# Score maxima as 128-row products with both groups first, block-diagonal expert keys, first expert product ordered by term

## The chip, the cores and the metric

The program runs on one core of one Trainium2 chip. The metric is the device time of one execution in microseconds (us). The engines are TensorE (PE, with its weight loads as PEld), VectorE (DVE), ScalarE (ACT), GpSimd (POOL) and SyncE (SP), each with an instruction queue of its own that runs in order, and DMA queues.

## What is computed

A two-layer diffusion backbone over 512 latent tokens and 256 context tokens, model width 1024. Cut to what matters here:

```python
for l in range(2):                      # layer 1 ("last") has latent queries only
    h = rms(x) * (1 + s1) + sh1         # modulated by c (latents) or c_ctx (context)
    q, k, v, u = split(h @ w_in[l])     # 8 query heads, 2 key heads, head width 64
    o_attn = softmax(q k^T / 8) v       # latents see context + latents, context sees context
    o_conv = silu(layer_norm(depthwise_conv31(glu(u))))
    x = x + g1 * concat(rms(o_attn), rms(o_conv)) @ w_o[l]
    h = rms(x) * (1 + s2) + sh2
    qp = (h @ w_pq[l]).reshape(T, 8, 2, 64)
    s = einsum('thcd,hckd->thck', qp, sub_keys)          # 2 halves x 128 keys
    i = top 16 of the 16 x 16 sums of the top 16 of each half   # of 16384 experts
    x = x + g2 * sum_e softmax(s_e) * gelu(h . U[e]) * V[e]     # 16 experts x 8 heads a token
return rms(x) * final_g
```

## The kernel before

Tokens lie on the columns: `xT[:, k, t]` holds 128 of the 1024 features of token t. A value that needs more than one pass of precision is split into a rounded part and a rest (`khh`/`klo`, `hhi`/`hlo`, `hi`/`lo`), and a product is the sum of two or three matmuls of the parts.

**Attention.** `att()` is one stream that a merge interleaves with the convolution's blocks (`convs`), the modulation products (`md`, tiles `mp`, `mps`) and the context's projection (`ctx`). For each group of queries, first the context tiles `CT`, then the latent tiles `LAT`, `largest` computes each query's largest score per head: for each head and span of keys one matmul L545 of `khh` over 128 rows and one L546 of `klo` over the lower 64 rows (`HD`), both into tile `s`, and a DVE reduction L547 into `nm`. `max_rows` turns `nm` into rows of `mT`, by way of `mh` on ACT. Then `attend` computes the probabilities from scores the other way round: `sT` is a matmul L435 of `khh` and a matmul L436 of `klo` with `qm`, both over 128 rows. The upper 64 rows of `klo` hold ones (L296), which in L436 subtract the maximum held in `mT`. The exponential is on ACT, the product with the values is `po` (L450). Of the convolution's 31 taps, DVE does some blocks (`L396`) and the pair ACT (`tp`, L399) and POOL (`yT`, L400) the others. `project_ctx` waits until the context's attention is done (`"att"`), and the output projection is `wo` (L676).

**Expert layer.** The 16384 experts are gone through densely for the larger part of the tokens, in 128 chunks a layer. `u_stream` loads a chunk (`raw`, SP's queue), rounds it on ACT (`hi`), takes the rest on POOL (`lo`), and runs 24 matmuls (`ups`, L963): 8 feature blocks times the three terms hi·hhi, hi·hlo, lo·hhi. GELU follows on ACT (`ge`), and the result is written out (`gd`). `v_stream` (`vps`, L1004) does the second product later. Beside `u_stream` run `queries` and `best16`: a projected query (`pq`, ring of tag `t2`) is multiplied with the `keys` (tile `sc`), whose two halves of 64 rows are two matmuls into two PSUM tiles, and DVE takes the 16 largest. `fg_stream` gathers single experts (`uv`) for the other tokens (L878 and L867 on DVE); `w_stream` builds the dense weights (`o`, `wps`).

**Order.** Streams are merged by clocks that add each step's estimated cost; a scheduler then places each engine's instructions in a fixed order in its queue.

Of the kernel before, what the change touches and what calls it, by code (L numbers as in the profile page):

```python
# [9 lines left out]
F32 = mybir.dt.float32  # L10
# [3 lines left out]
AF = mybir.ActivationFunctionType  # L14
# [3 lines left out]
P = 128  # L18
D = 1024
KD = D // P  # L20
SEQ = 512
CTX = 256
T = SEQ + CTX
NL = SEQ // P
NT = T // P
HD = 64
NQ = 8
NKV = 2
# [5 lines left out]
PH = 8  # L34
PK = 128
# [5 lines left out]
NEG = -3.0e38  # L41
# [19 lines left out]
def body(ctx: ExitStack, tc: tile.TileContext, io):  # L61
    nc = tc.nc
# [22 lines left out]
    V.memset(ones, 1.0)  # L85
    cT = per.tile([P, KD, 2], F32, name="cT")
    nc.sync.dma_start(cT, io["cT"])
    xT = per.tile([P, KD, T], F32, name="xT")
    x_src = io["xT"].rearrange("(k p) t -> p k t", p=P)
    for i in list(range(NL, NT)) + list(range(NL)):  # L90
# [9 lines left out]
    iota = per.tile([P, PK], F32, name="iota")  # L100
    V.tensor_copy(iota, iota_i)

    scT = per.tile([P, KD, 32], F32, name="scT")
    V.memset(scT, 0.0)
    A.activation(scT[:, :, 0:2], cT, AF.Silu)
    sel = per.tile([P, 2], F32, name="sel")
    V.tensor_tensor(out=sel, in0=ident[:, 0:2], in1=ident[:, 32:34], op=ALU.add)
    for g in (2, 3):
# [94 lines left out]
    def norm(tiles, hT, bc):  # L203

        t0, n = tiles[0] * P, len(tiles) * P
        for k in range(KD):
            V.tensor_tensor(out=hT[k], in0=xT[:, k, t0:t0 + n], in1=bc, op=ALU.mult)
# [22 lines left out]
    def attention_layer(l, st, fgs, fp, mark):  # L230
# [4 lines left out]
        last = l == 1  # L235
# [57 lines left out]
        klo = kp.tile([P, NKV, T], F32R, tag="klo", name="klo")  # L293
        vv = kp.tile([P, NT, NKV, HD + 1], F32, tag="vv", name="vv")
        V.memset(vv[:, :, :, HD:], 1.0)
        A.copy(klo[HD:], ones[HD:, 0:1].unsqueeze(2).to_broadcast([P - HD, NKV, T]))  # L296
        mT = kp.tile([P, nq * P], F32, tag="mT", name="mT")
        segs = [(0, SEQ, PAD)] if last else [(SEQ, CTX, LSEG + PAD), (0, SEQ, PAD)]
        gw = LSEG if last else GW
# [231 lines left out]
        def largest(g, kts, complete=True):  # L531

            k0, nk = kts[0] * P, len(kts) * P
            nh = max(1024 // nk, 1)
            for i in g:
                ts = slice(i * P, (i + 1) * P)
                nm = sm.tile([P, NQ], F32, tag="nm", name="nm", bufs=6)
                for h in range(0, NQ, nh):
                    ps = pbig.tile([P, 1024], F32, tag="big", name="s")
                    for j in range(nh):  # L540
                        for c in range(0, nk, 512):
                            n = min(512, nk - c)
                            ks = slice(k0 + c, k0 + c + n)
                            o = ps[:, j * nk + c:j * nk + c + n]
                            PE.matmul(o, qs[:, h + j, ts], khh[:, (h + j) % NKV, ks], start=True, stop=False)  # L545
                            PE.matmul(o, qs[0:HD, h + j, ts], klo[0:HD, (h + j) % NKV, ks], start=False, stop=True)  # L546
                    V.tensor_reduce(out=nm[:, h:h + nh], in_=ps[:, 0:nh * nk].rearrange("p (h k) -> p h k", k=nk), axis=AX.X, op=ALU.max, negate=True)  # L547
                    yield 0.9 * nh * nk / 768
                if i in part:
                    V.tensor_tensor(out=nm, in0=nm, in1=part[i], op=ALU.min)  # L550
                part[i] = nm
                if complete:
                    max_rows(i, nm)
# [82 lines left out]
        def att():  # L636
            if not last:
                yield from largest(CT, CT)
                yield from attend(CT, sp)
                done.append("att")  # L640
            yield from largest(LAT, CT[1:] if last else list(range(NT)))
            done.append("max")
            yield from attend(LAT, sp)

        def after_conv():
# [37 lines left out]
    def peer_layer(l, fp):  # L683
# [6 lines left out]
        with ExitStack() as outer:  # L690
# [19 lines left out]
            def best16(tiles, h, qT, keys, tmp):  # L710

                n = len(tiles)
                s = tmp.tile([P, 2, 2, PK], F32, tag="sc", name="sc", bufs=2)
                ps = [prt.tile([P, 2, PK], F32, tag="small", name="sc") for _ in range(2)]
                for c in range(2):
                    cs = slice(c * HD, (c + 1) * HD)
                    for j in range(n):
                        PE.matmul(ps[c][:, j, :], qT[cs, j * P:(j + 1) * P], keys[cs, h, :], start=True, stop=True)
                    A.copy(s[:, c, 0:n], ps[c][:, 0:n])
                for j, i in enumerate(tiles):  # L720
                    top, tix = tops[i]
                    for c in range(2):
                        V.max(out=top[:, h, c, 0:8], in_=s[:, c, j, :])
                        V.max_index(out=tix[:, h, c, 0:8], in_max=top[:, h, c, 0:8], in_values=s[:, c, j, :])
                        V.match_replace(out=s[:, c, j, :], in_to_replace=top[:, h, c, 0:8], in_values=s[:, c, j, :], imm_value=NEG)
                        V.max(out=top[:, h, c, 8:16], in_=s[:, c, j, :])
                        V.max_index(out=tix[:, h, c, 8:16], in_max=top[:, h, c, 8:16], in_values=s[:, c, j, :])

            def queries(g, hT, keys, tmp, first=False):

                n = len(g) * P
                todo = []
                for h in range(PH):
                    w = tmp.tile([P, KD, P], F32, tag="wq", name="wq", bufs=2)
                    nc.gpsimd.dma_start(w, io["peer_wq"][l][:, h * P:h * P + P].rearrange("(k p) n -> p k n", p=P))
                    ps = prt.tile([P, 512], F32, tag="small", name="pqp")
                    if len(hT) == 1:
                        terms = [(w, hT[0])]
                    else:
                        hi = tmp.tile([P, KD, P], F32R, tag="wqh", name="wqh", bufs=2)  # L740
                        lo = tmp.tile([P, KD, P], F32R, tag="wql", name="wql", bufs=2)
                        A.copy(hi, w)
                        G.tensor_tensor(out=lo, in0=w, in1=hi.bitcast(F32), op=ALU.subtract)
                        terms = [(hi, hT[0]), (hi, hT[1]), (lo, hT[0])]
                    for k in range(KD):
                        for m, (a, b) in enumerate(terms):
                            PE.matmul(ps[:, 0:n], a[:, k, :], b[k], start=k == 0 and m == 0, stop=k == KD - 1 and m == len(terms) - 1)
                    q = tmp.tile([P, 512], F32, tag="t2", name="pq", bufs=4)
                    A.copy(q[:, 0:n], ps[:, 0:n])
                    yield 1.0  # L750
                    todo.append((h, q))

                    while len(todo) > (1 if h < PH - 1 else 0):
                        done, q = todo.pop(0)
                        for j in range(0, len(g), 2):
                            best16(g[j:j + 2], done, q[:, j * P:], keys, tmp)
                            yield 2.0 * len(g[j:j + 2])
                        if first and (done + 1) % RH == 0:
                            yield from route(g[0], r2, done + 1 - RH, done + 1)
# [71 lines left out]
            def norm_fg(tmp):  # L831

                n = len(fgt) * P
                v = 0 if fgt[0] < NL else 1
                hT = []
                for _ in range((n + P) // (2 * P)):
                    t = fp.tile([P, 2 * D], F32, tag="g", name="hTf", bufs=4)
                    hT += [t[:, k * n:(k + 1) * n] for k in range(2 * D // n)]
                norm(fgt, hT, rms_rows(fgt, tmp, tag="t2", bufs=4) if l == 0 else rbc[:, td:])
                modulate(l, 1, v, hT)  # L840
                return hT

# [108 lines left out]
            def u_stream():  # L951

                for c in range(PK):
# [4 lines left out]
                    A.copy(hi, raw)  # L958
                    mark.append(G.tensor_tensor(out=lo, in0=raw, in1=hi.bitcast(F32), op=ALU.subtract))  # L959
                    ps = pdd[0].tile([P, 512], F32, tag="dd", name="ups")  # L960
                    for k in range(KD):
                        for n, (a, b) in enumerate(((hi, hhi), (hi, hlo), (lo, hhi))):
                            PE.matmul(ps[:, 0:td], a[:, k, :], b[:, k, :], start=k == 0 and n == 0, stop=k == KD - 1 and n == 2)  # L963
                    ge = up.tile([P, 512], F32, tag="ge", name="ge")
                    A.activation(ge[:, 0:td], ps[:, 0:td], AF.Gelu)  # L965
# [51 lines left out]
            us = u_stream()  # L1017
            fgs = fg_stream()
            with tc.tile_pool(name=f"tmp{l}", bufs=1, reuse_waits="tile") as tmp:
                keys = tmp.tile([P, PH, PK], F32, name="keys")  # L1020
                nc.sync.dma_start(keys, io["keys"][l])
                for i in fgt:
                    tops[i] = (tmp.tile([P, PH, 2, TOPK], F32, name=f"top{i}"), tmp.tile([P, PH, 2, TOPK], U32, name=f"tix{i}"))
                if l == 0:
                    hfg = norm_fg(tmp)
                for k in range(KD):
                    h = tmp.tile([P, 512], F32, tag="t2", name="xn", bufs=4)[:, 0:td]
                    V.tensor_tensor(out=h, in0=xT[:, k, 0:td], in1=rbc[:, 0:td], op=ALU.mult)
                    A.activation(h, h, AF.Identity, bias=mods[l, 3][:, k, 0:1], scale=mods[l, 4][:, k, 0:1])
                    A.copy(hhi[:, k, :], h)  # L1030
                    (G if k % 2 else V).tensor_tensor(out=hlo[:, k, :], in0=h, in1=hhi[:, k, :].bitcast(F32), op=ALU.subtract)  # L1031
# [124 lines left out]
```

## Time and profile before

| what | value |
|---|---|
| time, median of 3 runs | 4389.49 us (4384.52 to 4396.72) |
| the profiled execution: time, span | 4393.92 us, 4391.8 us |
| mean granted TensorE clock | 0.923 of full speed |
| busy: PE, PEld | 3982.1 us (91%), 3276.5 us (75%) |
| busy: DVE, POOL, ACT | 3110.9 us (71%), 2226.0 us (51%), 1901.0 us (43%) |

The span runs from the first to the last instruction of the profiled execution, 2.1 us less than its time, and that execution lies 4.4 us above the median. A busy share is a mean over stages that have different limits, and ends of pipelined matmuls are modelled, so that starts of successive matmuls tell their cost better than their durations.

### The profile page before, as it was taken

To read this page: it belongs to the slowest core of one execution; us is meant where nothing else is said; L and a number is where in the kernel's file an instruction comes from. 1 tells how busy PE (TensorE), PEld (TensorE's weight loads), DVE (VectorE), ACT (ScalarE), POOL (GpSimd) and SP (SyncE) were. 2 spreads that over 40 slices of the span, in tenths; PEclk is the share of its full clock that TensorE was granted. 3 is DMA by queue.
4 is the path that set the end of the run, shared out by engine and by line. 5 is a ranking of instruction groups with operands and counts; after the bars stand their busy time and mean duration, and the time that the engine had idled before them with its cause. 6 is when DMAs were issued, how large, how long until landed. Compare 5 with 4: busy or idle time off the path is not lost.

```text
span 4391.8 us, 54819 instructions
## 1 busy us (share of the span) xinstructions
PE 3982.1 (91%) x19512; PEld 3276.5 (75%) x19512; DVE 3110.9 (71%) x5700; ACT 1901.0 (43%) x3752; POOL 2226.0 (51%) x1231
## 2 busy tenths in 40 slices
PE   8879989999898998999999779889989889899998
PEld 5545857777787776888777535768878888889997
DVE  4683338999888657887877773349898553788886
ACT  3331432334777743333333243434367663333332
POOL 0551033657566455556555264136566455666664
PEclk9955989999999999999999875989999999999998
DMA  5132114797888898989887513226667778778885
GB/s 158 58 125 96 49 51 128 280 336 283 266 285 270 291 330 311 344 327 341 323 336 283 214 44 100 68 80 231 208 211 238 250 250 278 288 291 307 319 317 179
DMA packets 397921, 1003.75 MB, mean 229 GB/s; under 512 B 24400, under 2 KB 239696, under 8 KB 344400
## 3 DMA queue, kind: packets, MB, share of 16 engines
q1 hardware_dynamic: 330176, 577.10, 38.6%
q0 software_dynamic: 59904, 419.46, 25.9%
q10 hardware_dynamic: 7568, 3.70, 0.3%
q8 instruction: 154, 2.52, 0.2%
q14 instruction: 119, 0.97, 0.1%
HBM read 884.29 MB, written 115.87 MB: 228 GB/s over the span
## 4 chain that ended last, share of the span: by engine, by line
PE 37%; DVE 15%; DMA 11%; issue 5%; POOL 3%; ACT 2%; SPq 1%; POOLq 0%; ACTq 0%; DVEq 0%
PE vps L1004 19%; PE ups L963 8%; DMA raw<-in_uT 5%; DMA uv<-in_uv,uix 4%; DVE ge L939 2%; DVE alo L943 2%; PE wps L931 2%; DVE o L925 2%; POOL lo L959 2%; DMA vr<-in_vq 2%; DVE uv L878 1%; DVE yp L867 1%; PE wo L676 1%; PE s L546 1%; PE s L545 1%
## 5 line engine op out<-in xcount | busy, mean ns | idle before, releaser
L959 POOL TENSOR_TENSOR lo<-raw,hi 128x1024 fp32r<-128x1024 f32 x256 | 656.0, 2563 | 551.9 <-ACT hi L958 541.7
L997 POOL TENSOR_TENSOR vlo<-vr,vhi 128x1024 fp32r<-128x1024 f32 x256 | 632.4, 2478 | 476.6 <-ACT vhi L996 455.5
L963 PE MATMUL ups<-hhi,hi 128*128 128x512 f32 (+1 forms) x2048 | 773.8, 379 | 50.5 <-ACT ge L965 24.9
L963 PE MATMUL ups<-hhi,lo 128*128 128x512 f32 (+1 forms) x2048 | 775.7, 379 | 43.7 <-POOL lo L959 43.4
L1004 PE MATMUL vps<-ahi,vhi 128*128 128x512 f32 (+1 forms) x2048 | 756.7, 371 | 32.8 <-ACT vhi L996 19.3
L1004 PE MATMUL vps<-alo,vhi 128*128 128x512 f32 (+1 forms) x2048 | 759.2, 371 | 28.5 <-DVE alo L943 28.5
L963 PE MATMUL ups<-hlo,hi 128*128 128x512 f32 (+1 forms) x2048 | 767.4, 375 | 0.7 <-DVE hlo L1031 0.7
L1004 PE MATMUL vps<-ahi,vlo 128*128 128x512 f32 (+1 forms) x2048 | 750.0, 371 | 3.2 <-POOL vlo L997 3.2
L878 DVE SCALAR_TENSOR_TENSOR uv<-uv,hp 128x1024 f32<-128x1024 f32 x363 | 439.7, 1211 | 240.7 <-DMA uv<-in_uv,uix 240.3
L867 DVE SCALAR_TENSOR_TENSOR yp<-uv,act,yp 128x1024 f32<-128x1024 f32 x359 | 460.3, 1282 | 156.6 <-ACT act L880 151.9
L874 POOL DMA_INDIRECT uv<-in_uv,uix x384 | 434.2, 1131 | 211.7 <-DVE y L867 40.0
L963 PEld LDWEIGHTS ups<-hhi,lo 128*128 128x128 f32 x2048 | 397.4, 194 | 102.3 <-POOL lo L959 60.7
L963 PEld LDWEIGHTS ups<-hhi,hi 128*128 128x128 f32 x2048 | 398.6, 195 | 98.7 <-ACT ge L965 29.3
L1004 PEld LDWEIGHTS vps<-ahi,vhi 128*128 128x128 f32 x2048 | 390.2, 191 | 86.6 <-ACT vhi L996 19.9
L1004 PEld LDWEIGHTS vps<-alo,vhi 128*128 128x128 f32 x2048 | 390.9, 191 | 83.3 <-DVE alo L943 34.9
L1004 PEld LDWEIGHTS vps<-ahi,vlo 128*128 128x128 f32 x2048 | 390.2, 191 | 58.0 <-POOL vlo L997 6.8
L963 PEld LDWEIGHTS ups<-hlo,hi 128*128 128x128 f32 x2048 | 398.5, 195 | 42.7 <-DVE hlo L1031 1.5
L879 ACT ACTIVATE act<-dots 128x1 f32<-128x1 f32 x384 | 77.7, 202 | 790.0 <-DVE uv L878 783.0
L925 DVE TENSOR_TENSOR o<-iota,xf 128x1024 f32<-128x1024 f32 x224 | 375.5, 1698 | 29.7 <-PE wps L931 15.2
L400 POOL TENSOR_TENSOR yT<-yT,tp 128x512 f32<-128x512 f32 (+1 forms) x150 | 252.1, 1681 | 232.0 <-ACT tp L399 215.5
L996 ACT CAST vhi<-vr 128x1024 fp32r<-128x1024 f32 x256 | 266.1, 1045 | 218.6 <-PE vps L1004 103.0
L958 ACT CAST hi<-raw 128x1024 fp32r<-128x1024 f32 x256 | 267.3, 1045 | 186.5 <-DMA raw<-in_uT 97.9
(271 smaller groups left out, 6470.1 us busy)
## 6 DMA issues: line engine op xcount, KB each, us to landing
raw<-in_uT SPq DMA_DIRECT2D x256, 512.0 KB
vr<-in_vq SPq DMA_DIRECT2D x256, 512.0 KB
wd<-sg SPq DMA_DIRECT2D x28, 2048.0 KB
wm<-in_w_mod SPq DMA_DIRECT2D x48, 1024.0 KB
w<-wd SPq DMA_DIRECT2D x32, 1024.0 KB
gd<-ge SPq DMA_DIRECT2D x120, 256.0 KB
ge<-gd SPq DMA_DIRECT2D x60, 512.0 KB
w<-wd SPq DMA_DIRECT2D x32, 768.0 KB
```

The costliest lines, as they stand in the source:

```text
L400: G.tensor_tensor(out=y, in0=y, in1=tp, op=ALU.add)
L867: V.scalar_tensor_tensor(y, t[:, 1, :], act[:, e:e + 1], y, op0=ALU.mult, op1=ALU.add)
L874: got = G.indirect_dma_start(out=t.rearrange("p c d -> p (c d)"), out_offset=None, in_=io["uv"], in_offset=bass.IndirectOffsetOnAxis(ap=ui ...
L878: V.scalar_tensor_tensor(t[:, 0, :], t[:, 0, :], 1.0, at["h"], op0=ALU.mult, op1=ALU.mult, accum_out=dots[:, ec])
L925: V.tensor_tensor(out=oh, in0=iota.unsqueeze(1).unsqueeze(1).to_broadcast([P, 2, 4, PK]), in1=c2[:, :, tt].to_broadcast([P, 2, 4, PK]), op ...
L931: PE.matmul(ps[:, j, :], o1[:, j, :], o2[:, j, :], start=True, stop=True)
L958: A.copy(hi, raw)
L959: mark.append(G.tensor_tensor(out=lo, in0=raw, in1=hi.bitcast(F32), op=ALU.subtract))
L963: PE.matmul(ps[:, 0:td], a[:, k, :], b[:, k, :], start=k == 0 and n == 0, stop=k == KD - 1 and n == 2)
L996: A.copy(vhi, raw)
L997: mark.append(G.tensor_tensor(out=vlo, in0=raw, in1=vhi.bitcast(F32), op=ALU.subtract))
L1004: PE.matmul(ps[:, 0:td], a[:, c % 4, d * P:(d + 1) * P], b, start=c == 0 and n == 0, stop=c == 7 and n == 2)
```

## The change

1. The tile `scT` (SiLU of the two conditioning vectors) is filled before the input loads are issued from ACT's queue, and not after them.
2. `klo`'s upper 64 rows are first written as zeros; `largest` multiplies over all 128 rows in its second matmul too. In layer 0 both groups' maxima come first, then the upper rows are set to ones, then context and latents attend. In layer 1 the order of maxima and attention stays.
3. `keys` becomes block-diagonal: 128 rows, and for each head 256 columns, of which each half of the rows fills 128 and the others are zero. A tile of tokens then takes one matmul in place of two, with one PSUM tile and one copy for both halves. The ring `t2` has three buffers in place of four.
4. `u_stream` runs its 24 matmuls term by term, not feature block by feature block.

```diff
+    scT = per.tile([P, KD, 32], F32, name="scT")
+    V.memset(scT, 0.0)
+    A.activation(scT[:, :, 0:2], cT, AF.Silu)
     xT = per.tile([P, KD, T], F32, name="xT")
...
-    scT = per.tile([P, KD, 32], F32, name="scT")
-    V.memset(scT, 0.0)
-    A.activation(scT[:, :, 0:2], cT, AF.Silu)
...
-        A.copy(klo[HD:], ones[HD:, 0:1].unsqueeze(2).to_broadcast([P - HD, NKV, T]))
+        A.activation(klo[HD:], ones[HD:, 0:1].unsqueeze(2).to_broadcast([P - HD, NKV, T]), AF.Copy, scale=0.0)
...
-                            PE.matmul(o, qs[0:HD, h + j, ts], klo[0:HD, (h + j) % NKV, ks], start=False, stop=True)
+                            PE.matmul(o, qs[:, h + j, ts], klo[:, (h + j) % NKV, ks], start=False, stop=True)
...
             if not last:
                 yield from largest(CT, CT)
+            yield from largest(LAT, CT[1:] if last else list(range(NT)))
+            done.append("max")
+            A.copy(klo[HD:], ones[HD:, 0:1].unsqueeze(2).to_broadcast([P - HD, NKV, T]))
+            if not last:
                 yield from attend(CT, sp)
                 done.append("att")
-            yield from largest(LAT, CT[1:] if last else list(range(NT)))
-            done.append("max")
             yield from attend(LAT, sp)
...
-                ps = [prt.tile([P, 2, PK], F32, tag="small", name="sc") for _ in range(2)]
-                for c in range(2):
-                    cs = slice(c * HD, (c + 1) * HD)
-                    for j in range(n):
-                        PE.matmul(ps[c][:, j, :], qT[cs, j * P:(j + 1) * P], keys[cs, h, :], start=True, stop=True)
-                    A.copy(s[:, c, 0:n], ps[c][:, 0:n])
+                ps = prt.tile([P, 2, 2, PK], F32, tag="small", name="sc")
+                for j in range(n):
+                    PE.matmul(ps[:, j], qT[:, j * P:(j + 1) * P], keys[:, h], start=True, stop=True)
+                A.copy(s[:, 0:n], ps[:, 0:n])
...
-                    q = tmp.tile([P, 512], F32, tag="t2", name="pq", bufs=4)
+                    q = tmp.tile([P, 512], F32, tag="t2", name="pq", bufs=3)
...
-                    for k in range(KD):
-                        for n, (a, b) in enumerate(((hi, hhi), (hi, hlo), (lo, hhi))):
+                    for n, (a, b) in enumerate(((hi, hhi), (hi, hlo), (lo, hhi))):
+                        for k in range(KD):
                             PE.matmul(ps[:, 0:td], a[:, k, :], b[:, k, :], start=k == 0 and n == 0, stop=k == KD - 1 and n == 2)
...
-                keys = tmp.tile([P, PH, PK], F32, name="keys")
-                nc.sync.dma_start(keys, io["keys"][l])
+                keys = tmp.tile([P, PH, 2, PK], F32, name="keys")
+                for c in range(2):
+                    cs = slice(c * HD, (c + 1) * HD)
+                    V.memset(keys[cs, :, 1 - c], 0.0)
+                    nc.sync.dma_start(keys[cs, :, c], io["keys"][l][cs])
```

How the instructions move is shown at three places. A row is line, operation, output<-inputs and the output's shape; line numbers of the changed kernel are one higher at these places.

PE in layer 0, at the end of the context's maxima, before:

```order
L545 MATMUL s<-khh,qs 128x256
L546 MATMUL s<-klo,qs 128x256
L127 MATMUL mp_1283<-wm,scT 32x256 x8
L435 MATMUL sT<-qs,khh 128x256
L139 MATMUL mps<-sel,m_1292 128x2 x2
L127 MATMUL mp_1300<-wm,scT 32x256 x8
```

PE at the same place, in the changed kernel:

```order
L546 MATMUL s<-khh,qs 128x256
L547 MATMUL s<-klo,qs 128x256
L128 MATMUL mp_1283<-wm,scT 32x256 x8
L546 MATMUL s<-khh,qs 128x512
L547 MATMUL s<-klo,qs 128x512
L546 MATMUL s<-khh,qs 128x256
L547 MATMUL s<-klo,qs 128x256
L140 MATMUL mps<-sel,m_1292 128x2 x2
```

The context's attention (`sT` of 256 columns) no longer stands here: the latents' maxima follow at once, and the context's `sT` stand behind the last of them.

DVE in layer 0, from the last of the context's maxima on, before (`nm<-s 128x4` is a maximum of context queries, `128x1` of latent queries, `yT` a tap of the convolution):

```order
L547 TENSOR_REDUCE nm<-s 128x4
L396 SCALAR_TENSOR_TENSOR yT<-gp,convw,yT 128x798
L140 TENSOR_TENSOR mod_2_1246<-mps,bmod 128x4
L561 COPY ng<-mh 128x8
L562 TENSOR_TENSOR ng<-nm,mh 128x8
L396 SCALAR_TENSOR_TENSOR yT<-gp,convw,yT 128x798
L140 TENSOR_TENSOR mod_2_1246<-mps,bmod 128x4
L396 SCALAR_TENSOR_TENSOR yT<-gp,convw,yT 128x798 x2
```

DVE at the same place, in the changed kernel:

```order
L548 TENSOR_REDUCE nm<-s 128x4
L548 TENSOR_REDUCE nm<-s 128x1
L397 SCALAR_TENSOR_TENSOR yT<-gp,convw,yT 128x798
L141 TENSOR_TENSOR mod_2_1246<-mps,bmod 128x4
L562 COPY ng<-mh 128x8
L563 TENSOR_TENSOR ng<-nm,mh 128x8
L548 TENSOR_REDUCE nm<-s 128x1
L397 SCALAR_TENSOR_TENSOR yT<-gp,convw,yT 128x798
L548 TENSOR_REDUCE nm<-s 128x1
```

The taps, which stood in one run with no latent maximum between them, now alternate with the 32 latent maxima, and the last taps stand behind the last maximum.

PE in the expert layer's first product, layer 0, before (`htp` is another stream's transposition):

```order
L1041 MATMUL htp<-ident,hTf 128x128 x8
L963 MATMUL ups<-hhi,hi 128x512
L963 MATMUL ups<-hlo,hi 128x512
L963 MATMUL ups<-hhi,lo 128x512
L963 MATMUL ups<-hhi,hi 128x512
```

PE there in the changed kernel:

```order
L1046 MATMUL htp<-ident,hTf 128x128 x4
L964 MATMUL ups<-hhi,hi 128x512 x8
L964 MATMUL ups<-hlo,hi 128x512 x6
L1046 MATMUL htp<-ident,hTf 128x128 x4
L964 MATMUL ups<-hlo,hi 128x512 x2
L964 MATMUL ups<-hhi,lo 128x512 x6
```

The first matmul that reads `lo` was the third of a chunk's 24 and is now the seventeenth; the last that reads `hi` was the twenty-third and is now the sixteenth.

## Rows read from the trace of the kernel before

**Rows 1.** The page: share of the chain that ended last, by line.

```profile
PE vps L1004 19%; PE ups L963 8%; DMA raw<-in_uT 5%; DMA uv<-in_uv,uix 4%; DVE ge L939 2%; DVE alo L943 2%; PE wps L931 2%; DVE o L925 2%; POOL lo L959 2%; DMA vr<-in_vq 2%; DVE uv L878 1%; DVE yp L867 1%; PE wo L676 1%; PE s L546 1%; PE s L545 1%
```

**Rows 2.** Windows: length, busy time (x instructions) by engine, PEclk, DMA share, GB/s.

```profile
200.00:300.00 100.00, 72.33 (x323) 39.66 (x323) 92.89 (x72) 33.99 (x48) 62.50 (x34) 0.59 0.43 137
300.00:400.00 100.00, 96.57 (x241) 52.82 (x237) 43.67 (x76) 19.08 (x31) 28.35 (x18) 0.50 0.10 32
2627.00:2727.00 100.00, 98.69 (x298) 55.37 (x296) 33.50 (x59) 24.99 (x46) 37.45 (x27) 0.57 0.29 95
640.00:1680.00 1040.00, 955.66 (x4609) 780.72 (x4608) 851.30 (x2013) 580.42 (x1270) 587.21 (x320) 0.97 0.80 270
2900.00:3770.00 870.00, 763.67 (x4353) 722.75 (x4353) 612.83 (x1348) 470.07 (x997) 493.63 (x247) 0.95 0.69 231
700.00:1000.00 300.00, 285.13 (x1268) 224.99 (x1267) 296.87 (x1193) 109.97 (x227) 173.84 (x109) 0.98 0.76 268
```

**Rows 3.** Timeline, layer 0, one latent head's maximum: start, duration, engine, operation, idle before.

```profile
342.42 0.79 PE L545 MATMUL s<-khh,qs 128*128 128x512 f32 x1
...
343.87 0.58 PE L545 MATMUL s<-khh,qs 128*128 128x256 f32 x1
...
344.89 0.79 PE L545 MATMUL s<-khh,qs 128*128 128x512 f32 x1
345.00 0.96 DVE L547 TENSOR_REDUCE nm<-s 128x1 f32<-128x768 f32 x1 [1.51 <-PE s L546]
```

**Rows 4.** Timeline of PE, context's attention: scores by 128-row matmuls alone.

```profile
278.57 0.63 PE L436 MATMUL sT<-qm,klo 128*128 128x256 f32 x2
278.99 0.41 PE L435 MATMUL sT<-qs,khh 128*128 128x256 f32 x1
```

**Rows 5.** Timeline of PE, latents' attention in layer 0: its steady start, then later.

```profile
430.84 0.63 PE L435 MATMUL sT<-qs,khh 128*128 128x512 f32 x1
431.27 0.83 PE L436 MATMUL sT<-qm,klo 128*128 128x512 f32 x2
...
470.57 0.39 PE L435 MATMUL sT<-qs,khh 128*128 128x512 f32 x1
470.81 0.39 PE L436 MATMUL sT<-qm,klo 128*128 128x512 f32 x1
```

**Rows 6.** Timeline of PE, layer 0: end of the context's maxima, start of the latents'.

```profile
252.94 0.58 PE L546 MATMUL s<-klo,qs 64*128 64x256 f32 x1
...
308.58 0.79 PE L545 MATMUL s<-khh,qs 128*128 128x512 f32 x1 [0.47 <-ACT p L438]
```

**Rows 7.** Groups on DVE from 236 to 430 us: count, busy, mean ns, idle before.

```profile
L396 DVE SCALAR_TENSOR_TENSOR yT<-gp,convw,yT 128x798 f32<-128x798 f32 x30 | 46.5, 1551 | 0.5
L547 DVE TENSOR_REDUCE nm<-s 128x1 f32<-128x768 f32 x32 | 30.6, 958 | 55.2 <-PE s L546 55.2
```

**Rows 8.** Timeline of PE, layer 1: a pair of 128 columns, one of 512, the next.

```profile
2680.26 0.47 PE L545 MATMUL s<-khh,qs 128*128 128x128 f32 x1
...
2681.07 0.79 PE L545 MATMUL s<-khh,qs 128*128 128x512 f32 x1
...
2682.52 0.47 PE L545 MATMUL s<-khh,qs 128*128 128x128 f32 x1
```

**Rows 9.** Timeline, layer 1: last taps on POOL, convolution's result on ACT, output projection.

```profile
2741.44 9.69 POOL L400 TENSOR_TENSOR yT<-yT,tp 128x512 f32<-128x512 f32 x7 [0.23 <-ACT tp L399]
...
2820.53 1.28 ACT L522 CAST yhi<-yf 128x512 fp32r<-128x512 f32 x2 [1.42 <-DVE yf L519]
...
2827.40 0.48 PE L676 MATMUL wo<-yhi,w 128*128 128x512 f32 x1
```

**Rows 10.** Who waited for tile `lo` (us, times).

```profile
  PE ups L963: 43.4, 36
```

**Rows 11.** Who waited for tile `ups` (us, times).

```profile
  ACT hi L958: 69.2, 38
```

**Rows 12.** Timeline of PE, expert layer: products `pqp` of 256 columns, `sc` of two token tiles.

```profile
661.66 4.48 PE L747 MATMUL pqp<-hTf,wq 128*128 128x256 f32 x20
...
762.79 0.71 PE L718 MATMUL sc<-keys,pq 64*128 64x128 f32 x4
```

More of the change, by code (lines that the diff above doesn't have):

```diff
@@ L722, in best16 @@
                     for c in range(2):
[L723 to L727, printed above, removed]
+                        V.max(out=top[:, h, c, 0:8], in_=s[:, j, c, :])
+                        V.max_index(out=tix[:, h, c, 0:8], in_max=top[:, h, c, 0:8], in_values=s[:, j, c, :])
+                        V.match_replace(out=s[:, j, c, :], in_to_replace=top[:, h, c, 0:8], in_values=s[:, j, c, :], imm_value=NEG)
+                        V.max(out=top[:, h, c, 8:16], in_=s[:, j, c, :])
+                        V.max_index(out=tix[:, h, c, 8:16], in_max=top[:, h, c, 8:16], in_values=s[:, j, c, :])
             def queries(g, hT, keys, tmp, first=False):
@@ L838, in norm_fg @@
                     hT += [t[:, k * n:(k + 1) * n] for k in range(2 * D // n)]
-                norm(fgt, hT, rms_rows(fgt, tmp, tag="t2", bufs=4) if l == 0 else rbc[:, td:])
+                norm(fgt, hT, rms_rows(fgt, tmp, tag="t2", bufs=3) if l == 0 else rbc[:, td:])
                 modulate(l, 1, v, hT)
@@ L1026, in peer_layer @@
                 for k in range(KD):
-                    h = tmp.tile([P, 512], F32, tag="t2", name="xn", bufs=4)[:, 0:td]
+                    h = tmp.tile([P, 512], F32, tag="t2", name="xn", bufs=3)[:, 0:td]
                     V.tensor_tensor(out=h, in0=xT[:, k, 0:td], in1=rbc[:, 0:td], op=ALU.mult)
```

## The prediction

> **What bounds the kernel now.** The page's chain [rows 1] comes first: the expert layer's second product (`vps`) is 19% of it, the first (`ups`) 8% and its loads `raw` 5%, while the score maxima (`s`) are 1% a line. Most of the change touches lines that the chain hardly names, so each stage has to be read by itself.
>
> Windows [rows 2] show two such stages. From 300 to 400 us (layer 0) and from 2627 to 2727 us (layer 1) PE counts as 97 and 99% busy at a granted clock of 0.50 and 0.57, with DVE at 44 and 34 us of 100 and the DMA queues at 10 and 29%. PE sets the pace there, and the timeline shows with what. One latent head's maximum [rows 3] goes 342.42, 343.87, 344.89: 1.45 us for a pair (khh, klo) of 512 columns and 1.02 us for one of 256, 2.47 us a head, after which DVE reduces in 0.96 us and has waited 1.51 us for PE. The same kind of score product stands in the context's attention [rows 4], where both matmuls use 128 rows: two of 256 columns start at 278.57 and the next at 278.99, 0.21 us each, a pair 0.42 us. With 512 columns [rows 5] the spacing is 0.43 us (430.84 to 431.27) at the low level of the clock and 0.24 us at the high one (470.57 to 470.81). So with a 64-row partner a pair costs 0.6 us more than with a 128-row one, at either width: 0.3 us at each passage between 128 and 64 rows, whatever is streamed. That is the price to be removed.
>
> Of the first expert product, windows [rows 2] say that PE is busy 956 of 1040 us in layer 0 and 764 of 870 in layer 1: 84 and 106 us are all the idle time that a better order can win. The row of who waited for `lo` [rows 10] gives 43.4 us of it, in 36 waits. `hi` on ACT waits 69.2 us for `ups` [rows 11], since the old buffer is read up to the twenty-third matmul of 24.
>
> **The change part by part.** *Maxima, layer 0.* There are 32 latent heads (8 heads by 4 tiles): 32 x 2.47 = 79 us now. With 128 rows at the low clock a head is 2 x 0.43 + 0.42 = 1.28 us, together 41 us: 38 us less on PE. Further, the latents' maxima now start behind the context's at 253 us and not at 308.6 [rows 6]. From 200 to 300 us PE is busy 72 of 100 [rows 2], so some 14 of those 55 us are holes, which the maxima can fill. DVE's queue then has 30 taps (mean 1.55 us) and 32 maxima (0.96 us) in alternation, 77 us [rows 7], and could be done by 253 + 77 = 330 us or, with its smaller work, some 20 us later; the steady part of the latents' attention starts at 431 us now [rows 5]. PE is the later of the two: 431 - 38 = 393 us with no hole filled, 379 with all of them. The gain is 38 to 52 us; I take 45. Its bounds: nothing, if PE and DVE take turns (1.28 + 0.96 + 1.55 = 3.8 us a head, 121 us from 253 to 374, and the context's attention, the 55 us between 253 and 308.6, after that: 429); and, should the clock be granted in full, 41 us become half, and the gain 72.
>
> The context's attention now waits for all maxima. Behind it stand the context's projection and the second part of the convolution's norms; the output projection needs the latents' attention, which ends later than they in both orders. The refill of `klo` with ones is one ACT copy in each layer, short beside the stretch that it closes; its zeroing takes the place of the copy at the start. I cost both at nothing, and at 3 us if ACT is late. In layer 1 only the copy is new.
>
> *Maxima, layer 1.* 32 pairs of 512 columns and 64 of 128 (32 heads by 640 keys, and 32 by 128 before). A pair of 128 takes 0.81 us and one of 512 takes 1.45 us [rows 8]: 52 + 46 = 98 us. After: 0.86 us for 512 columns; for 128 no 128-row pair is on record, so it is bounded by the whole and the half of a 256-column pair, 0.42 and 0.21 us. Sum 41 to 55 us, gain 43 to 57. I take 45, near the lower end, since the first passes lie among other work. But the convolution may be next in line: POOL's taps end at 2751 us, the result `yhi` comes at 2822 and the output projection starts at 2827.4 [rows 9]. If POOL gets no earlier, `wo` wins only 5 us. It should get earlier, as its partner ACT is held behind a copy of the maxima, which come sooner. Bounds 5 and, with the full clock, 72.
>
> *Term order.* A chunk's first 16 matmuls (16 x 0.24 = 3.8 us by the spacing at the high level [rows 5]) no longer need `lo`, and `hi` comes free eight matmuls earlier. All 43.4 us of waiting for `lo` can go; what else runs beside it (DVE 82% and DMA 80% busy in layer 0, 70 and 69% in layer 1 [rows 2]) will take part of it back, as neither gets faster. I take 25; bounds 0, and 60 if the other idle time shrinks with it.
>
> *Keys.* For two token tiles there were four instructions of 128 columns, 0.71 us [rows 12]; now there are four of 256, of which the trace has another product's at 4.48 / 20 = 0.22 us, 0.9 us. With 48 such groups PE pays 10 us more, less 0.6 us for each two passages between 64 and 128 rows that go: a gain of at most 19 us, a loss of at most 10. One ACT copy takes the place of two. In layer 0 these stand where DVE is busy 297 of 300 us [rows 2], so neither PE nor ACT decides there. I take nothing. The two small memsets and the split load come where DVE and SP wait for the output projection.
>
> The Trainium skill speaks against this part. TensorE: Matmul & The Clock Gate, section "Why this matters for your kernels", says that matmuls over fewer than 128 rows in distinct row groups run at the same time. By it the two old halves would have cost as one, and the new form twice as much. The four instructions in 0.71 us do not look so: side by side they would have fitted into half of a full-width 0.9 us. By the rule the part loses 48 x 0.45 = 22 us of PE time, by the row about nothing.
>
> *SiLU at the queue's head.* The input loads fill the start either way, and PE's next work needs the squares of the loaded input. Nothing, at most 3 us to either side.
>
> Sum: 45 + 45 + 25 = 115 us. The profiled execution took 4393.9 us and lies 4.4 above the median of 4389.5, so 4393.9 - 115 - 4.4 = 4274.5 us against that median.
>
> **The rivals.**
> 1. *The term order yields nothing*, because loads and DVE set the pace of the expert layer. For it: `raw` is 5% of the chain [rows 1]. Against: PE waits for `lo` by name. Gain 90: 4299 us.
> 2. *The convolution takes the maxima's place.* In layer 0 DVE's taps and maxima go in turn (gain 0), or in layer 1 POOL's end stands (gain 5). For it: `yhi` ends 5 us before `wo` [rows 9]; against: DVE waits 55 us for PE ahead of its maxima [rows 7]. One of them: 4314 to 4319; both: 4359.
> 3. *The clock rises.* Dense maxima may be granted the high level, as the attention after 470 us is [rows 5]. Gain 72 + 72 + 25: 4220 us. Against: with DVE in the way PE has gaps in layer 0.
> 4. *Products side by side*, the skill's rule above, and nothing hides it: 4274 + 22 = 4296 us.
> 5. *Slower: the ring of three.* `pq` has one buffer less. If the next projection (24 matmuls by 0.24 = 5.8 us) has to wait until the last `sc` is done, DVE stands still in a stage in which it is busy 99% [rows 2]. 32 projections by 5.8 us are 186 us, and the time is 4274 + 186 = 4460. It decides from 3.6 us a projection on. Against it: the code holds one `pq` back, works on one and writes one, which is three.
>
> **How the numbers follow.** Likeliest, with its own range of 4240 to 4295 us: 4274, chance 0.50. Rival 1: 0.15. Rival 2: 0.17, a third of it with both layers. Rival 3: 0.10. Rival 4: 0.02. Rival 5: 0.06, of which half ends slower than before and half eats most of the gain. Runs of this kernel differ by 0.3%, 12 us, and less can't be told from no change. Faster: 0.91; same, from rival 2 with 1 together and from the weak rival 5: 0.05; slower: 0.04. The range goes from rival 3's 4215, its faster half left out, to 4330, which leaves out rival 2 with both layers and rival 5.
>
> **What would show it.** Right: `s` pairs of 512 columns 0.86 us apart or less with a klo of 128*128, the latents' steady `sT` near 385 us, layer 1's maxima some 45 us shorter and `wo` starting as much earlier; PE's wait for `lo` under 10 us. Wrong: pairs still 0.3 us a matmul apart (then the rows are not the cause); DVE full between 253 and 390 us and PE waiting for `nm`; `wo` waiting for `yhi` in layer 1; the first expert product as long as before with `raw`, `ge` or `hi` in `lo`'s place; DVE waiting for `sc` or `pq`.

## The result and the profile after

The changed kernel takes 4239.3 us (median of 4 runs, 4227.3 to 4246.3) against 4390.1 us, a ratio of 0.9653 with a 95% interval of 0.9627 to 0.9679: 151 us less, where 115 were forecast. The time lies in the range of the prediction (4215 to 4330 us), 35 us below its likeliest value and at the lower edge of that case's own range (4240 to 4295).

The starts of each stage's first and last matmuls divide the two profiled executions into stages (4391.8 and 4239.3 us of span):

| stage | before | after | difference |
|---|---|---|---|
| start to the first score maximum, layer 0 | 222.9 | 216.6 | -6.3 |
| maxima and attention to the first `ups`, layer 0 | 406.9 | 330.8 | -76.1 |
| first to last `ups`, layer 0 | 1036.4 | 1041.4 | +5.0 |
| last `ups` to last `vps`, layer 0 | 756.5 | 749.4 | -7.1 |
| last `vps` to the first maximum of layer 1 | 152.4 | 140.7 | -11.7 |
| maxima and attention to the first `ups`, layer 1 | 347.3 | 284.9 | -62.4 |
| first to last `ups`, layer 1 | 835.5 | 838.2 | +2.7 |
| last `ups` of layer 1 to the end | 633.9 | 637.3 | +3.4 |

The first product's stages, on which a third term of the prediction rested, are no shorter; the two attention stages give 138 us. The 12 and 7 us of the stages around the second product were not traced to a part. The windows over the maxima of the changed kernel, from the first to the last of each layer (length, busy by engine, clock, DMA):

```profile
216.00:314.00 98.00, 63.60 (x449) 44.64 (x437) 96.17 (x94) 37.25 (x56) 76.84 (x38) 0.83 0.52 169
2479.00:2558.00 79.00, 66.29 (x375) 45.53 (x375) 58.45 (x85) 39.71 (x69) 64.94 (x46) 0.91 0.41 134
```

The same stretches took 184 and 152 us before. In layer 0 PE was busy 159 of those 184 us at a clock of 0.51 (97% at 0.50 in its middle, [rows 2]) and is now busy 64 of 98 us at 0.83: less busy and at a higher granted clock. In layer 0 DVE, with 96 of 98 us, now sets the pace. The timeline of one latent head there (start, duration, engine, operation, idle before), to be read against [rows 3]:

```profile
280.20 0.94 DVE L548 TENSOR_REDUCE nm<-s 128x1 f32<-128x768 f32 x1
...
280.26 0.50 PE L546 MATMUL s<-khh,qs 128*128 128x512 f32 x1 [1.19 <-DVE nm L548]
...
280.60 0.39 PE L547 MATMUL s<-klo,qs 128*128 128x512 f32 x1
...
280.83 0.28 PE L546 MATMUL s<-khh,qs 128*128 128x256 f32 x1
...
280.95 0.28 PE L547 MATMUL s<-klo,qs 128*128 128x256 f32 x1
281.07 1.03 DVE L397 SCALAR_TENSOR_TENSOR yT<-gp,convw,yT 128x798 f32<-128x798 f32 x1
...
281.20 0.50 PE L546 MATMUL s<-khh,qs 128*128 128x512 f32 x1
```

A pair of 512 columns takes 0.57 us (280.26 to 280.83) where it took 1.45. The next head starts after 0.94 us here, but that is not the pace: the first of the 32 heads starts at 243.5 us and the last at 313.2, 2.2 us apart on average, since DVE alternates their maxima with taps. PE now waits for DVE (`nm`, 15.8 us in 11 waits), not DVE for PE. The groups on DVE from 234 to 316 us say the same (idle before, at the end, against 55.2 us in [rows 7]):

```profile
L397 DVE SCALAR_TENSOR_TENSOR yT<-gp,convw,yT 128x798 f32<-128x798 f32 x26 | 40.9, 1575 | 0.0
L548 DVE TENSOR_REDUCE nm<-s 128x1 f32<-128x768 f32 x32 | 29.9, 946 | 1.4 <-PE s L547 1.3
```

In layer 1 the pairs of 512 and 128 columns, against [rows 8]:

```profile
2540.05 0.49 PE L546 MATMUL s<-khh,qs 128*128 128x512 f32 x1
...
2540.60 0.22 PE L546 MATMUL s<-khh,qs 128*128 128x128 f32 x1
...
2541.12 0.53 PE L546 MATMUL s<-khh,qs 128*128 128x512 f32 x1 [0.19 <-DVE nm L548]
```

1.07 us for both, a wait for DVE included, where it was 2.26. The convolution came along, as its rows in the timeline show against [rows 9]:

```profile
2589.85 4.07 POOL L401 TENSOR_TENSOR yT<-yT,tp 128x512 f32<-128x512 f32 x3
...
2659.52 1.28 ACT L523 CAST yhi<-yf 128x512 fp32r<-128x512 f32 x2 [1.42 <-DVE yf L520]
...
2668.22 0.48 PE L679 MATMUL wo<-yhi,w 128*128 128x512 f32 x1
```

POOL's last taps end at 2594 us instead of 2751, and `wo` starts 7 us after `yhi`, as before some 5 us after it.

Of the first product, the changed kernel's row of PE's side among those who waited for `lo`, against [rows 10]:

```profile
  PEld ups L964: 1.0, 3
```

Only its weight loads are left there, with 1.0 us (60.7 us in 54 waits before, beside the 43.4 us of the matmuls). PE's waits in the first product's stage of layer 1, in the changed kernel (us, times, longest):

```profile
PE wps L932 <- ACT sg L933: 40.7, 17, 6.0
PE ups L964 <- ACT hi L959: 18.8, 5, 5.5
PE ups L964 <- ACT ge L966: 17.8, 10, 4.7
```

and before:

```profile
PE ups L963 <- POOL lo L959: 22.4, 22, 2.1
PE ups L963 <- ACT hi L958: 20.6, 8, 6.1
PE wps L931 <- ACT sg L932: 17.4, 14, 3.0
PE ups L963 <- ACT ge L965: 10.7, 5, 3.7
```

The wait for `lo` has become a wait for what stands in ACT's queue (`sg` are the copies of the dense weights). Over both layers the waits for `sg`, `o`, `act` and `ge` rise from 74 to 131 us (122 in a second profile of the changed kernel), while 43 us for `lo` go. ACT's own wait in front of `hi` has moved too: the group of `hi`, after and before, says what ended its idle time:

```profile
L959 ACT CAST hi<-raw 128x1024 fp32r<-128x1024 f32 x256 | 267.6, 1046 | 235.6 <-DMA raw<-in_uT 211.4 <-PE ups L964 20.8 <-POOL lo L960 2.1
```

```profile
L958 ACT CAST hi<-raw 128x1024 fp32r<-128x1024 f32 x256 | 267.3, 1045 | 186.5 <-DMA raw<-in_uT 97.9 <-PE ups L963 69.2 <-issue 15.3
```

`hi`'s buffer is free sooner (69.2 to 20.8 us), but ACT then stands before a load that has not landed, with `sg`, `o` and `ge` behind it.

### The profile page after: what moved, and what is told of

It reads as the page before. It is cut to its first block, busy times and chain, and to the rows that moved or that the text cites. A ratio compares the mean times of both kernels' runs of the same rounds, so it can differ in the third digit from the quotient of the medians.

```text
span 4239.3 us, 54433 instructions
## 1 busy us (share of the span) xinstructions
PE 3809.7 (90%) x19352; PEld 3225.7 (76%) x19352; DVE 3087.0 (73%) x5704; ACT 1900.3 (45%) x3704; POOL 2231.8 (53%) x1231
## 5 line engine op out<-in xcount | busy, mean ns | idle before, releaser
L960 POOL TENSOR_TENSOR lo<-raw,hi 128x1024 fp32r<-128x1024 f32 x256 | 640.0, 2502 | 595.2 <-ACT hi L959 531.2
L1005 PE MATMUL vps<-ahi,vhi 128*128 128x512 f32 (+1 forms) x2048 | 756.5, 371 | 23.0 <-ACT vhi L997 16.2
L964 PE MATMUL ups<-hhi,hi 128*128 128x512 f32 (+1 forms) x2048 | 509.9, 387 | 68.4 <-ACT ge L966 39.5
L964 PE MATMUL ups<-hhi,lo 128*128 128x512 f32 (+1 forms) x2048 | 477.9, 370 | 0.1
L964 PEld LDWEIGHTS ups<-hhi,hi 128*128 128x128 f32 x2048 | 385.9, 199 | 120.1 <-ACT ge L966 47.8
L964 PE MATMUL ups<-hlo,hi 128*128 128x512 f32 (+1 forms) x2048 | 476.9, 370 | 0.0
L964 PEld LDWEIGHTS ups<-hlo,hi 128*128 128x128 f32 x2048 | 378.2, 192 | 39.5
L964 PEld LDWEIGHTS ups<-hhi,lo 128*128 128x128 f32 x2048 | 372.1, 190 | 39.2 <-POOL lo L960 1.0
L932 PE MATMUL wps<-o 128*128 128x128 f32 x1792 | 265.3, 295 | 89.8 <-ACT sg L933 55.4
```

What stands on the lines that cost most here:

```text
L932: PE.matmul(ps[:, j, :], o1[:, j, :], o2[:, j, :], start=True, stop=True)
L1005: PE.matmul(ps[:, 0:td], a[:, c % 4, d * P:(d + 1) * P], b, start=c == 0 and n == 0, stop=c == 7 and n == 2)
```

## The experiments

The theory to be tried: the passages between 64 and 128 rows cost the time of the maxima and hold the clock low, and the order only lets the maxima fill holes; the term order moves PE's wait from POOL to ACT's queue; keys and SiLU do nothing. Rivals stand in each expectation. Ratios are to the kernel before, run beside each kernel on the same chip; they and not the medians are compared. A per cent is 44 us.

| run | median, us | ratio, 95% interval |
|---|---|---|
| the changed kernel again | 4234.9 | 0.9655 (0.9631 to 0.9679) |
| old term order | 4256.5 | 0.9697 (0.9675 to 0.9720) |
| old keys | 4239.6 | 0.9650 (0.9629 to 0.9672) |
| late SiLU | 4247.2 | 0.9682 (0.9658 to 0.9706) |
| 64 rows | 4347.5 | 0.9906 (0.9876 to 0.9936) |
| old order of the maxima | 4247.4 | 0.9664 (0.9647 to 0.9681) |
| half loads | 4225.1 | 0.9603 (0.9575 to 0.9632) |
| half loads, old term order | 4233.4 | 0.9652 (0.9619 to 0.9685) |
| no scaling of `o` | 4194.9 | 0.9556 (0.9530 to 0.9583) |
| no scaling of `o`, old term order | 4260.1 | 0.9703 (0.9678 to 0.9728) |
| before, maxima's part alone | 4266.0 | 0.9706 (0.9686 to 0.9727) |
| before, term order alone | 4370.1 | 0.9948 (0.9928 to 0.9967) |

**The changed kernel again.** 

> The changed kernel itself once more, as the yardstick of the runs beside it. Both theories expect 4239 us, within 10 us.

As expected. Its two profiles also say how far a stage of one execution can be trusted: the first product of layer 1 took 838.2 us in one and 824.6 in the other, the start 216.6 and 222.2.

**64 rows in the new order.**

```diff
-PE.matmul(o, qs[:, h + j, ts], klo[:, (h + j) % NKV, ks], start=False, stop=True)
+PE.matmul(o, qs[0:HD, h + j, ts], klo[0:HD, (h + j) % NKV, ks], start=False, stop=True)
```

> The changed kernel with the maxima's second matmul over 64 rows again, in the new order. Theory (the passages between 64 and 128 rows cost the time, and hold the clock low): pairs of 512 columns 1.45 us apart again, clock near 0.5 while the maxima run, layer 1 back to some 150 us between its first and last maximum and its gain of 72 us lost; of layer 0's 76 us only the filled holes, some 15, are kept. Time 4350 to 4380 us. Rival (the new order and what runs beside it raised the clock): under 4290 us.

Measured 4347 us, just under the expected 4350: 110 us (0.9906 - 0.9655, 17 to either side) of the 151 are lost by this one line. The windows over the maxima show the low clock again:

```profile
218.00:362.00 144.00, 133.86 (x433) 66.07 (x432) 95.70 (x96) 38.53 (x58) 72.04 (x39) 0.51 0.36 117
2532.00:2668.00 136.00, 126.14 (x373) 69.11 (x373) 58.32 (x85) 40.91 (x72) 65.92 (x47) 0.64 0.24 78
```

and its timeline in layer 1 the old spacing, 1.45 us a pair of 512 columns:

```profile
2640.35 0.79 PE L546 MATMUL s<-khh,qs 128*128 128x512 f32 x1
2641.07 0.79 PE L547 MATMUL s<-klo,qs 64*128 64x512 f32 x1
2641.80 0.47 PE L546 MATMUL s<-khh,qs 128*128 128x128 f32 x1
```

Layer 0's attention stage is 375.1 us here, so the order alone is worth 32 us of 406.9, twice what was expected; the theory holds for layer 1 (345.3 us against 347.3 before).

For the clock it holds only in part. In layer 1 of this run, with modulation products (`mp`) between the heads, the clock was granted in full for 16 us although the rows alternated, and a pair of 512 columns then took 0.87 us (a window first, then its timeline):

```profile
2587.60:2604.00 16.40, 16.40 (x104) 9.39 (x104) 7.09 (x13) 7.99 (x14) 11.24 (x10) 1.00 0.86 278
2587.68 0.50 PE L546 MATMUL s<-khh,qs 128*128 128x512 f32 x1
...
2588.55 0.33 PE L546 MATMUL s<-khh,qs 128*128 128x128 f32 x1
```

The fourth case, full rows at the low level, stands in the changed kernel, in a stretch from 295.6 to 299 us with a clock of 0.50:

```profile
297.59 0.63 PE L546 MATMUL s<-khh,qs 128*128 128x512 f32 x1
...
298.44 0.41 PE L546 MATMUL s<-khh,qs 128*128 128x256 f32 x1
```

That is 0.85 us. So of the fall from 1.45 to 0.57 us a pair, the rows give 0.60 at the same clock, and the clock the other 0.28.

**128 rows with the old order of layer 0.**

```diff
             if not last:
                 yield from largest(CT, CT)
+                fill(1.0)
+                yield from attend(CT, sp)
+                done.append("att")
+                fill(0.0)
             yield from largest(LAT, CT[1:] if last else list(range(NT)))
             done.append("max")
-            A.copy(klo[HD:], ones[HD:, 0:1].unsqueeze(2).to_broadcast([P - HD, NKV, T]))
-            if not last:
-                yield from attend(CT, sp)
-                done.append("att")
+            fill(1.0)
             yield from attend(LAT, sp)
```

`fill(x)` writes x into `klo`'s upper rows on ACT. 

> The changed kernel with 128 rows, but in layer 0 the latents' maxima behind the context's attention again; klo's upper rows are filled with ones, zeros and ones in turn. Theory (the rows are the gain, the order only fills the holes of 253 to 308 us): 14 us for the holes and 2 to 5 for the fills lost, 4250 to 4260 us. Rival (putting the maxima first is worth as much as the rows): 30 us or more lost, over 4270 us.

Measured 4247 us; its attention stage of layer 0 takes 345.8 us against 330.8 and 332.7 in the two runs of the changed kernel: 13 to 15 us for the order, fills included. In the time itself the difference (0.0009 from the changed kernel's second run, 4 us) is inside the intervals. By the stages, the rows come first: once they are full, the order adds 14 us; with 64 rows it had added 32.

**The maxima's part alone**, on the kernel before: the edits of `klo`, `largest` and `att()` in the change's diff. 

> The kernel before with the maxima's part of the change alone: 128 rows, both groups first, refill of klo. Theory (the other three parts are worth some 10 to 20 us together): attention's stages as in the changed kernel, 4245 to 4260 us. Rival (the other parts cancel out): 4237 us, within 8.

Measured 0.9706: 129 us with an interval of 9 to either side. The attention stages are 331.8 and 296.0 us. So some 22 us (14 to either side) are left for the other parts together, at the upper end of what was expected.

**The term order alone**, on the kernel before: the swap of the two loops. 

> The kernel before with the term order alone. Theory (the wait for lo goes, the wait for ACT's queue comes): 5 to 18 us faster than before, 4372 to 4385 us. Rival 1 (the prediction's term): 25 us faster, 4365 us. Rival 2 (nothing): 4390 us, within 5.

Measured 0.9948 (0.9928 to 0.9967): 23 us, 9 to either side. That is near the prediction's 25, rival 1 of this run; the theory's upper end of 18 lies inside the interval too.

**The old term order** in the changed kernel, the same swap undone. 

> The changed kernel with the first product's 24 matmuls feature block by feature block again. Theory (the term order only moves the waits: the first product's two stages took 1036 and 836 us before and 1041 and 838 us after): within 8 us of the changed kernel, 4231 to 4247 us, and PE waiting for lo again by some 40 us. Rival (the term order brings the 25 us of the prediction and something else of the change eats them): 25 us slower than the changed kernel, about 4264 us.

Measured 0.9697 against 0.9655: 18 us, 14 to either side. PE waits 43.3 us for `lo` again. So the order is not worth nothing, though the 8 us that the theory allowed lie inside the interval. But little of it shows in the first product: its stages take 1051.4 and 830.5 us, against 1041.4 and 838.2 or 1042.9 and 824.6. The attention of layer 1, which the edit does not touch, takes 301.3 us against 284.9 and 285.7. The order of instructions in that stage differs between the two kernels (it is the same in the two runs of the changed kernel), since the scheduler decides it for the whole program; that this is the cause was not tried.

**The old keys**: both matmuls of 64 rows, two tiles and copies, ring of four, as in the diff's minus lines. 

> The changed kernel with the keys in two halves of 64 rows again, two PSUM tiles, two copies, and the ring of four. Theory (the block-diagonal keys do nothing): within 8 us of the changed kernel. Rival 1 (the ring of three and the wider products cost time, and hide a gain of the term order): 15 to 25 us faster, about 4220 us. Rival 2 (the fewer passages between 64 and 128 rows are a gain): 10 to 19 us slower.

Measured 0.9650 against 0.9655: nothing, within 14 us. What the two forms cost PE has to be read anew, since the row in [rows 12] is not the whole work of two token tiles. The old form takes eight instructions for them, four for each half of the rows (320 in all, against 160 in the changed kernel), and [rows 12] shows one half. In the kernel before the halves mostly stand apart, as two rows of four with 0.71 us each; here they stand together:

```profile
756.70 0.72 PE L718 MATMUL sc<-keys,pq 64*128 64x128 f32 x8
757.35 0.50 PE L963 MATMUL ups<-hhi,hi 128*128 128x512 f32 x1
```

and in the changed kernel the new form:

```profile
766.95 1.09 PE L719 MATMUL sc<-keys,pq 128*128 128x256 f32 x4
767.69 1.05 PE L964 MATMUL ups<-hhi,hi 128*128 128x512 f32 x3
```

From start to next start the new form takes 0.74 us, the two halves together 0.65, and two halves apart 0.64 each (762.79 to 763.43 in the kernel before). So for PE the full-width form is little dearer where the halves stood together and cheaper where they stood apart, and the time shows neither. The Trainium skill says in TensorE: Matmul & The Clock Gate, section "Why this matters for your kernels", that matmuls over few rows in distinct row groups run at the same time. The rows agree, with eight instructions in 0.72 us where four take 0.71; the doubling that the prediction worked out from the rule does not show.

**Late SiLU**, the three lines of `scT` put back. 

> The changed kernel with the SiLU behind the input loads in ACT's queue again. The first qkv matmul started at 49.8 us before and at 43.7 us after. Theory (the early SiLU lets PE begin with the squares' sums, and the clock rises 20 us sooner): the first qkv near 50 us and the time 6 us longer, 4245 us. Rival (the 6 us come from elsewhere): first qkv near 44 us, 4239 us.

Measured 0.9682 against 0.9655, 12 us with 15 to either side: undecided by the time. The theory's sign does not show: the first `qkv` started at 46.8 us here, and at 43.7 and 49.0 us in the two runs of the changed kernel. The start varies by as much without the edit, so the 6 us of the first table are no effect that can be told from it.

**Half loads.**

```diff
-                    raw = up.tile([P, KD, P], F32, tag="raw", name="raw", bufs=2)
-                    nc.sync.dma_start(raw, io["uT"][l, c])
+                    raw = up.tile([P, KD // 2, P], F32, tag="raw", name="raw", bufs=2)
+                    nc.sync.dma_start(raw, io["uT"][l, c][:, 0:KD // 2])
...
-                    A.copy(hi, raw)
+                    both = raw.rearrange("p k t -> p (k t)").unsqueeze(1).to_broadcast([P, 2, KD * P // 2])
+                    A.copy(hi.rearrange("p (a k) t -> p a (k t)", a=2), both)
```

POOL's `lo` reads `both` in the same way. 

> The changed kernel with half of the first product's load: each chunk brings four feature blocks of eight, which ACT and POOL read twice (the other four are left out of the product, all else runs as before). Theory (ACT's queue, in which hi, sg, o, act and ge stand one behind the other, sets PE's waits, and the loads do not): the two stages stay at 1041 and 838 us within 15 us each, 4220 to 4245 us. Rival (loads set the pace): 60 us shorter or more, under 4180 us.

Measured 4225 us, 23 us (16 to either side) less; the stages are 1039.0 and 806.8 us. In layer 0 the loads are not the pace, in layer 1 they are some 20 to 30 us of it; the 60 us of the rival are not there. The 20 to 30 us rest on one profile of this run, and layer 1's stage differed by 14 us between two profiles of the changed kernel.

**Half loads in the old term order.** 

> The same with the feature blocks in the old order. Theory: 43 us of waiting for lo in place of the waits for sg, o and ge, and the time within 20 us of the other run with half loads. Rival (with the loads out of the way the term order earns its 25 us or more): 25 to 45 us slower than that run.

0.9652 against 0.9603, 22 us with 19 to either side, and 8 us by the medians: undecided between the theory's "within 20" and the rival's "25 to 45". PE waits 38 us for `lo` here.

**No scaling of `o`.**

```diff
-                                A.activation(o2[:, j, :], o2[:, j, :], AF.Copy, scale=wT[:, t:t + 1])
```

> The changed kernel without the 896 ACT instructions that scale o by the routing weights (the dense weights are then 0 or 1; some 349 us of ACT's work less, 0.39 us each). Theory (ACT's queue sets PE's waits in the first product now): the waits for sg, o, act and ge fall from about 129 us to under 65, and the two stages (1041 and 825 to 838 us) lose 30 to 70 us together; 4170 to 4210 us. Rival (DVE or the loads set the pace, and ACT only shows it): the time stays within 15 us, 4222 to 4252 us.

Measured 0.9556 against 0.9655: 43 us, 16 to either side. PE's waits for `sg`, `act` and `ge` are 57 us, and the two stages take 1027.0 and 795.9 us. `o` now comes straight from DVE, and the waits for it are 38 us; with them the sum is 95 us and not under 65 as expected. Still, the waits for `sg` and `ge`, whose own work did not change, fell from 95 to 48 us: much of what PE waited for was ACT's queue.

**No scaling of `o`, old term order.** 

> The same with the feature blocks in the old order. Theory: once ACT is relieved, the wait for lo is a loss by itself, and this run is 25 to 43 us slower than the other one without the scaling. Rival (the wait for lo is covered in any case): within 15 us of it.

0.9703: 65 us (16 to either side) slower than with the new order, and no faster than the changed kernel in the old order with ACT's work whole (0.9697). PE waits 37.8 us for `lo` here. With the old order ACT's relief is worth nothing, and with ACT relieved the new order is worth 65 us instead of 18, more than the 25 to 43 expected: each of the two gains was covered while the other wait stood. Of the 65 us, 53 lie in the first product's stages (1058.2 and 818.2 us against 1027.0 and 795.9) and 15 in the attention of layer 1 (299.5 against 284.6), the same 15 or 16 that the old order cost there with ACT's work whole.

## Why the prediction was right, and where it was off

**What bounded the maxima.** Right, and shown: the one line with 64 rows gives back 110 us. The Trainium skill says in TensorEngine Tiling (Array Packing), section "Key Properties", that a change of tiling mode drains TensorE; the rows agree, with 0.3 us at each passage at the low clock (1.45 against 0.85 us a pair).

**Layer 0: 45 us forecast, 76 in the profile, 75 with the maxima's part alone.** The mechanism held; the size failed in one step. The sum took 1.28 us a head, from the low clock's 0.43 and 0.21 us a matmul. A head took 0.81 us of PE (0.69 from its first to its last start, 280.26 to 280.95, and 0.12 for the last) at a clock of 0.83, though PE had gaps: rival 3, which got 0.10, with its argument "against" wrong. The measured 4239 us lie nearer to that rival's 4220 than to the likeliest 4274. The full-clock bound, 72, was nearly the measured value. The step "PE is the later of the two" failed with it, since over the maxima DVE set the pace (96 of 98 us). DVE full and PE waiting for `nm`, put down as a mark of failure if it lasted to 390 us, did come, but ended at 314. The latents' attention then ran steadily from 362 us, not 385, in the changed kernel's timeline against [rows 5]:

```profile
361.78 0.50 PE L436 MATMUL sT<-qs,khh 128*128 128x512 f32 x1 [0.52 <-ACT p L439]
362.12 0.39 PE L437 MATMUL sT<-qm,klo 128*128 128x512 f32 x1
```

Rival 2's turn-taking did not come, since the head's 0.94 us on DVE overlapped PE.

**Layer 1: 45 forecast, 51 with the maxima's part alone, 62 in the whole change.** The 51 lie in the forecast's 43 to 57. In the whole change the maxima's stretch fell by 73 us (151.3 to 78.8), again the full-clock bound, and 10 us came back behind it: PE's wait for `qm` from DVE grew there from 0.6 to 6.5 us, and the cause of the rest is open. Why the whole change gains 11 us more here is open too; with the old term order the stage gains 46. That the convolution would follow, and not hold `wo`, was right.

**Term order: 25 forecast, 23 alone, 18 in the whole.** That about half of the 43 us is taken back by what runs beside it was right in size, but not by its reason: what takes it back is ACT's queue, where the sum named DVE and DMA. The prediction's own mark of failure, the first product as long as before with `raw`, `ge` or `hi` in `lo`'s place, is what the profile of the whole change shows for PE's waits (`ge`, and `sg` in the same queue). Of the 18 us, some 16 stand in the attention of layer 1 by the profiles, where the prediction had nothing. So that 25 came close is in part luck.

**Keys: nothing, and nothing measured.** The sum behind it was misread: it took the row of one half for the whole of two token tiles, so its 10 us more for PE were no cost of the new form, and its argument against products side by side had no ground. They do run side by side where the halves stand together, and still the rival's loss of 22 us did not come, as the full-width form took 0.74 us and not twice 0.65. **Ring of three:** with the ring of four again (in the old keys) the time was the same, so the slower rival did not come. **SiLU:** nothing forecast, nothing that could be told.

The sum of the parts as measured alone (75 + 51 + 23 = 149) meets the measured 151; where in the program they gain is less settled, as said of layer 1.

## What to carry to other kernels

Read the start-to-start spacing of matmuls, not their busy share: at 97% busy a pair took 1.45 us that full rows do in 0.85 at the same clock. Where two alternating products use different numbers of rows, pad the narrower one with zeros to full rows; it was worth 110 us where the narrow ones stood between wide ones, and nothing in the time for the keys. Before a row is taken for the price of a form, count its instructions against the code: half of a group was read as the whole here. And before moving a wait, look at what stands behind the next one in an in-order queue: the term order's gain was 18 us with ACT's queue full and 65 with it relieved.

## What was not expected of the hardware

The granted clock did not follow the counted busy share: 0.51 over layer 0's maxima with PE counted busy for 134 of 144 us and 64-row partners, 0.83 with 64 of 98 us and full rows. Alternating rows alone do not hold it low either: with modulation products between the heads it was 1.00 for 16 us of the run with 64 rows. Which property of the matmuls kept it low was not separated. And full rows at the low level and 64-row partners at the high one cost the same, 0.85 and 0.87 us a pair: here the passages cost about as much as the fall of the clock to its low level.
